# Beginning of a two-layer trunk: the first feature's modulation weights issued by ScalarE's queue beside SyncE's x tiles, the forget bias loaded behind the second half of x

## The chip, the core and the metric

The kernel runs on one core of a Trainium2 chip. The metric is device time in microseconds (us) of one launch.

## The reference

The trunk has two layers of width 1024 over 1024 tokens, all in float32. Layer 0 mixes tokens with forgetting attention, layer 1 with gated linear attention; each is followed by a SwiGLU. What stands at the beginning:

```
c_act = jax.nn.silu(c)
mod = c_act @ ada_w[i] + ada_b[i]
sh1, sc1, g1, sh2, sc2, g2 = jnp.split(mod, N_MOD, axis=-1)
h = modulate(rms_norm(x, norm1_g[i]), sh1, sc1)      # h * (1 + sc1) + sh1
proj = h @ w_in
q, k, v, f_logit = jnp.split(proj, [D, 2 * D, 3 * D], axis=-1)
log_f = jax.nn.log_sigmoid(f_logit + b_f)
cum = jnp.cumsum(log_f, axis=1).transpose(0, 2, 1)
```

So the first thing on TensorE that is of any size, the projections of layer 0, needs the normalised and modulated x, and this needs x, c, and shift and scale, which are products of c with 8 MB of `ada_w` (two blocks of 1024 x 1024).

## The kernel before

Every large matrix product is done as three: operands are split into a high and a low part (a cast on ScalarE for the high one, a subtraction on VectorE or GpSimd for the low one), and `mm3` (L240) issues high x high (L241), high x low (L242) and low x high (L243). The instructions of each engine stand in an order that a scheduler has chosen from its own model of the run; the code's order, priorities and the reuse of buffers bound it. So a change in the order of the code can move instructions on all engines.

**Tiles.** "Feature" d (0 to 7) is a block of 128 of the 1024 features; x tiles t (0 to 7) are blocks of 128 tokens, 512 KB each. The tokens are done in two halves: tiles 0 to 3 first, 4 to 7 next.

**Loads at the beginning.** `load_x` (L279) loads an x tile. `load_ada0(d)` (L284) loads what feature d needs of `ada_w`: two tiles `adas`, one for each half of the rows, each by two transfers of 256 KB (L288). c is loaded twice: as rows (L298) with other small vectors (L299 to L306), to be transposed by TensorE, and four times as a block of 32 x 32 (L294, `craw`) for later modulations (`cblk`, L325). `bf`, the forget bias (L311), is 64 bytes. `load_w16` (L215) loads the 16 columns of the forget logits, `load_w` (L198) a projection weight of 512 KB and splits it (L206 high on ScalarE, L209 low on GpSimd and VectorE). `ada_pair` (L361) loads, 128 KB at a time, what later modulations need.

**Queues.** SyncE (SP) issues all of these but the four blocks of c, which ScalarE (ACT) issues. The transfers of both engines take eight completion semaphores in turn, DMAHW0 to DMAHW7, in the order in which the scheduler places them: a transfer waits, on the engine that issues it, until the previous one on its semaphore has landed. An engine issues its transfers in its order, and on ScalarE arithmetic stands in the same order behind them.

**The first half.** `ss_half(0)` squares x (L458, ScalarE), makes the row scales and scales x (L469). For each d, `pre(d)` (L840) calls `ada0_mod(d)` (L474), `load_ada0(d + 3)` and `h_block(d, 0)`. `ada0_mod` forms shift and scale of a feature: for d = 0 to 2 four of the eight row blocks are products on TensorE (L481) and four accumulate on VectorE (L487, L489), for d = 3 to 7 all eight on VectorE; two matmuls with ones (L491, `mp`) sum the accumulated tile over its partitions; L492 and L342 turn the sum into `modc` and `amul`. `h_block` (L495) transposes x (L498, `xp`), modulates it on ScalarE (L500, `y`), casts the high part there (L502) and takes the low part (L503) on VectorE for even d, GpSimd for odd d. `first_k` (L508) does the forget logits (L510, L511, `fs`), and the first query and key projections (`qs`, `ks`); `first_v` (L829) the values (`vps`).

**Between the halves.** At d = 4 the loads of x tiles 4 to 7 are written, then `ss_half(1)`. `first_evac(0)` (L799) takes the logits out of PSUM (L223), applies bias, absolute value, exponential and, behind the second half, logarithm and a scan along the tokens; `v_split` (L163, L164) splits the values; `h_block(d, 1)` and `first_k(d, 1)` do the second half. The scan's result goes to memory and back, and attention starts with it.

Of the kernel before, what the change touches and what calls it, by code (L numbers as in the profile page):

```python
# [53 lines left out]
def trunk(ctx, tc, x, c, ada_w, ada_b, norm1_g, norm2_g, ffn_w_in, ffn_w_out,  # L54
          fox_w_in, fox_b_f, fox_w_out, gla_w_in, gla_w_a2, gla_b_a, gla_g_o,
          gla_w_out, final_g, out, dbg=None, stop=None):
    nc = tc.nc
# [51 lines left out]
    def psl(t, n=1):  # L109
        return slice(t * P, (t + n) * P)  # L110
# [167 lines left out]
    def load_x(t):  # L278
        nc.sync.dma_start(xt[t], x[0, psl(t), :])  # L279

    adaw = ada_w.rearrange("l (k p) (j d m) -> l p k j d m", p=P, j=6, m=P)
    araw = {}

    def load_ada0(d):  # L284
        for kh in range(2):
            t = adr([P, 4, 2, P], F32, f"adas{d}{kh}")
            for j in range(2):
                nc.sync.dma_start(t[:, :, j, :], adaw[0, :, 4 * kh:4 * kh + 4, j, d, :])  # L288
            araw[(d, kh)] = t

    craw = mrows[4][:, 0:32]
    cblk = cst.tile([P, 32], F32, name="cblk")
    for q in range(4):
        nc.scalar.dma_start(craw[32 * q:32 * q + 32], c[0].rearrange("(r s) -> r s", s=32))  # L294
    load_x(0)
    rows2 = mrows[1][0:32]
    nc.vector.memset(rows2, 0.0)
# [8 lines left out]
    nc.sync.dma_start(rows[112:128, :], norm2_g.rearrange("l (j p) -> (l j) p", p=P))  # L306
    load_x(2)
    load_x(3)
    load_ada0(0)
    bf = cst.tile([16, 1], F32, name="bf")  # L310
    nc.sync.dma_start(bf, fox_b_f.rearrange("o h -> h o"))  # L311
    W = fox_w_in[0]
    wf = load_w16(W[:, 3 * D:3 * D + 16], "fw", wst)
    wq0 = load_w(W[:, 0:P], "wq0", wst)
    wk0 = load_w(W[:, D:D + P], "wk0", wst)
    load_ada0(1)
    load_ada0(2)

    vps = mp0([P, 160], F32, "vps")
# [135 lines left out]
    def ss_half(hf):  # L455
        for t in range(4 * hf, 4 * hf + 4):
            sq = sqr([P, D], BF16, f"sq{t}")
            nc.scalar.activation(sq, xt[t], AF.Square, accum_out=ssx[:, t:t + 1])  # L458
        cs = slice(4 * hf, 4 * hf + 4)
        nc.vector.tensor_scalar(rstd[:, cs], ssx[:, cs], 1.0 / D, EPS, op0=ALU.mult, op1=ALU.add)  # L460
        nc.gpsimd.tensor_tensor(rstd[:, cs], rstd[:, cs], mhalf[:, 0:4], op=ALU.pow)
        for t in range(4 * hf, 4 * hf + 4):
            r = rstd[:, t:t + 1]
            if hf == 0 and t % 2 == 0:
                nc.vector.tensor_scalar(xt[t], xt[t], r, None, op0=ALU.mult)
            elif hf == 0 and t == 1:
                nc.scalar.activation(xt[t], xt[t], AF.Copy, scale=r)
            else:
                nc.gpsimd.tensor_scalar(xt[t], xt[t], r, 1.0, op0=ALU.mult, op1=ALU.mult)  # L469
# [38 lines left out]
    def first_k(d, hf, acc):  # L508
        ps = acc[0][1]
        nc.tensor.matmul(ps, wf[:, d, :], hT[d].hi[:, hsl(hf)], start=d == 0, stop=False)  # L510
        nc.tensor.matmul(ps, wf[:, d, :], hT[d].lo[:, hsl(hf)], start=False, stop=d == 7)  # L511
        for w, ps in acc[1:]:
            mm3(ps, w.hi[:, d, :], w.lo[:, d, :], hT[d].hi[:, hsl(hf)], hT[d].lo[:, hsl(hf)], d == 0, d == 7)
# [316 lines left out]
    def first_v(d):  # L830
        wv = wvs[0][d // 4]
        for tp in range(2):
            for i in range(2):
                ts_ = psl(2 * tp + i)
                p_, a_ = vacc[tp][:, i, :], (hT[d].hi[:, ts_], hT[d].lo[:, ts_])
                nc.tensor.matmul(p_, a_[0], wv.hi[:, d % 4, :], start=d == 0 and i == 0, stop=False)
                nc.tensor.matmul(p_, a_[0], wv.lo[:, d % 4, :], start=False, stop=False)
                nc.tensor.matmul(p_, a_[1], wv.hi[:, d % 4, :], start=False, stop=d == 7 and i == 1)

    def pre(d):  # L840
        ada0_mod(d)
        if d + 3 < 8:
            load_ada0(d + 3)
        h_block(d, 0)

    pre(0)
    for d in range(8):
        if d == 0:
            feed.depth = 1
            wvs[0] = [feed.next()]  # L850
        if d == 2:
            wvs[0].append(feed.next())
        if d < 7:
            pre(d + 1)
        first_k(d, 0, acc)
        if d >= VLAG:
            first_v(d - VLAG)
        if d == XD:
            for t in range(4, 8):
                load_x(t)  # L860
            ss_half(1)
    for d in range(8 - VLAG, 8):
        first_v(d)
# [1085 lines left out]
```

## Time and profile before

| | us |
|---|---|
| median of 3 runs | 2429.87 |
| lowest, highest | 2428.5, 2430.59 |
| profiled execution, its time | 2430.71 |
| its span | 2429.0 |
| TensorE busy | 2375.2 (98%) |
| VectorE busy | 1689.5 (70%) |
| ScalarE busy | 1192.6 (49%) |
| GpSimd busy | 1164.0 (48%) |

The span runs from the first to the last instruction that the profiler recorded. The mean granted clock of TensorE in it was 0.992 of full speed. In rows of the order of time, the columns are start and length (us), engine, line, operation, what is written and read by the program's names (buffer numbers left out), shape and count; in brackets how long the engine had waited, and for what. "SPq" is SyncE's queue of transfers, "PE" is TensorE. In rows by stretches of time the columns are the stretch, its sum, busy time and instructions of PE, its weight loads, VectorE (DVE), ScalarE (ACT) and GpSimd (POOL), then the granted clock of TensorE, the mean busy share of the DMA engines (of which more than one can count in a stretch that transfers enter and leave) and GB/s.

### The profile page before, as it was taken

What the parts mean: (1) busy time and instruction counts of PE and PEld (TensorE: products, weight loads), DVE (VectorE), ACT (ScalarE), POOL (GpSimd) and SP (SyncE); (2) the same over time, 40 slices, a digit from 0 to 9 for tenths busy, and PEclk for the clock granted to TensorE, in tenths of its full rate; (3) what the DMA queues carried; (4) which work ended last, traced back from release to release, by engine and by line L of the source; (5) the groups of instructions that cost most, each with busy time, mean ns of one, the idle gap of its engine ahead of it and who ended that gap; (6) DMA issues with size and microseconds to landing.
All of it is one profiled execution on the core that took longest, in us unless ns stands there. A gap on an engine that the chain in (4) does not pass through costs nothing.

```text
span 2429.0 us, 36104 instructions
## 1 busy us (share of the span) xinstructions
PE 2375.2 (98%) x12338; PEld 2019.5 (83%) x12338; DVE 1689.5 (70%) x2845; ACT 1192.6 (49%) x2286; POOL 1164.0 (48%) x1015
## 2 busy tenths in 40 slices
PE   7999999999999999999999999999999999999998
PEld 6788888878888888888888798898888888888888
DVE  6578777676687777766788545436587767666787
ACT  4656556666544444445324756654343334345325
POOL 3333333333337878753363544552335656653362
PEclk9999999999999999999999999999999999999999
DMA  9233333123326555457665334444325434347664
GB/s 271 80 105 113 94 108 113 62 88 120 118 96 192 180 167 171 156 187 262 229 204 168 83 114 117 126 126 156 109 84 186 152 135 155 128 169 258 231 209 148
DMA packets 329503, 362.40 MB, mean 149 GB/s; under 512 B 24476, under 2 KB 252984, under 8 KB 329320
## 3 DMA queue, kind: packets, MB, share of 16 engines
q1 hardware_dynamic: 329128, 360.09, 46.2%
q8 instruction: 97, 1.59, 0.3%
q14 instruction: 86, 0.70, 0.1%
q10 hardware_dynamic: 192, 0.02, 0.0%
HBM read 269.78 MB, written 90.24 MB: 148 GB/s over the span
## 4 chain that ended last, share of the span: by engine, by line
PE 78%; DVE 6%; DMA 6%; ACT 3%; issue 2%; POOL 2%; SPq 2%; DVEq 0%; POOLq 0%; ACTq 0%
PE p_b L241 16%; PE p_b L243 16%; PE p_b L242 16%; PE o_b L968 2%; PE t_b L954 2%; SPq L361 1%; DMA ad_s<-in_ada_w_dram 1%; PE qk_b L241 1%; PE qk_b L242 1%; PE qk_b L243 1%; DMA ada_s<-in_ada_w_dram 1%; PE s_b L923 1%; PE s_b L924 1%; PE vps_b L241 1%; PE vps_b L242 1%
## 5 line engine op out<-in xcount | busy, mean ns | idle before, releaser
L164 DVE TENSOR_TENSOR o_s<-xv_s,o_s 128x512 fp32r<-128x512 f32 (+1 forms) x376 | 333.4, 890 | 82.3 <-ACT o_s L163 81.3
L163 ACT CAST o_s<-xv_s 128x512 fp32r<-128x512 f32 (+1 forms) x376 | 217.9, 586 | 319.5 <-PE p_b L243 250.8
L934 POOL TENSOR_SCALAR lp_s<-lp_s,st 128x128 f32<-128x128 f32 (+7 forms) x128 | 98.5, 775 | 291.1 <-DVE st L933 273.1
L242 PE MATMUL p_b<-B,o_s 128*128 128x512 f32 x608 | 237.8, 391 | 0.0
L243 PE MATMUL p_b<-B,o_s 128*128 128x512 f32 x608 | 237.2, 391 | 0.0
L241 PE MATMUL p_b<-B,o_s 128*128 128x512 f32 x608 | 236.6, 392 | 0.0
L702 POOL TENSOR_TENSOR ex_s<-xv_s,xv_s 128x512 f32<-128x512 f32 (+1 forms) x64 | 86.4, 1350 | 270.2 <-DMA xv_s<-in_ffn_w_in_dram 108.3
L241 PE MATMUL p_b<-T,o_s 128*128 128x512 f32 x480 | 186.7, 389 | 0.0
L242 PE MATMUL p_b<-T,o_s 128*128 128x512 f32 x480 | 186.7, 389 | 0.0
L243 PE MATMUL p_b<-T,o_s 128*128 128x512 f32 x480 | 180.7, 389 | 0.0
L932 ACT ACTIVATE lp_s<-lp_s,st 128x128 f32<-128x128 f32 (+7 forms) x128 | 99.3, 776 | 76.7 <-DVE st L928 73.9
L241 PEld LDWEIGHTS p_b<-B,o_s 128*128 128x128 f32 x608 | 115.0, 189 | 23.8
L243 PEld LDWEIGHTS p_b<-B,o_s 128*128 128x128 f32 x608 | 114.7, 189 | 24.0
L242 PEld LDWEIGHTS p_b<-B,o_s 128*128 128x128 f32 x608 | 114.9, 189 | 23.7
L1306 DVE TENSOR_TENSOR ex_s<-ex_s,p_b 128x512 f32<-128x512 f32 x140 | 93.6, 680 | 31.8 <-PE p_b L243 31.7
L704 POOL TENSOR_TENSOR xv_s<-ex_s,xv_s 128x512 f32<-128x512 f32 (+1 forms) x64 | 85.9, 1342 | 52.3 <-DVE o_s L164 49.7
L163 ACT CAST pt_s<-t_b 128x512 fp32r<-128x512 f32 (+1 forms) x160 | 79.9, 548 | 62.5 <-PE t_b L954 61.6
L243 PEld LDWEIGHTS p_b<-T,o_s 128*128 128x128 f32 x480 | 90.1, 188 | 18.8
L241 PEld LDWEIGHTS p_b<-T,o_s 128*128 128x128 f32 x480 | 90.1, 188 | 18.7
L242 PEld LDWEIGHTS p_b<-T,o_s 128*128 128x128 f32 x480 | 90.1, 188 | 18.6
L164 DVE TENSOR_TENSOR pt_s<-t_b,pt_s 128x512 fp32r<-128x512 f32 (+1 forms) x160 | 96.5, 631 | 11.4 <-ACT pt_s L163 10.8
L968 PE MATMUL o_b<-pt_s,v_s 128*128 128x256 f32 x512 | 95.6, 295 | 5.9 <-DVE pt_s L164 4.2
(1950 smaller groups left out, 7494.7 us busy)
## 6 DMA issues: line engine op xcount, KB each, us to landing
xv_s<-in_ffn_w_in_dram SPq DMA_DIRECT2D x176, 256.0 KB, 3.3
hid_B<-x SPq DMA_DIRECT2D x70, 512.0 KB, 2.8
ad_s<-in_ada_w_dram SPq DMA_DIRECT2D x384, 64.0 KB, 2.0
hid_T<-x SPq DMA_DIRECT2D x36, 512.0 KB, 2.8
xv_s<-in_ffn_w_out_dram SPq DMA_DIRECT2D x96, 192.0 KB, 5.1
ada_s<-in_ada_w_dram SPq DMA_DIRECT2D x128, 128.0 KB, 2.7
xv_s<-in_ffn_w_out_dram SPq DMA_DIRECT2D x40, 256.0 KB, 2.8
T2o<-hid_T SPq DMA_DIRECT2D x18, 512.0 KB, 9.0
```

The costliest lines, as they stand in the source:

```text
L163: nc.scalar.copy(hi, src)
L164: nc.vector.tensor_sub(lo, src, hi.bitcast(F32))
L241: nc.tensor.matmul(ps, ah, bh, start=start, stop=False)
L242: nc.tensor.matmul(ps, ah, bl, start=False, stop=False)
L243: nc.tensor.matmul(ps, al, bh, start=False, stop=stop)
L702: nc.gpsimd.tensor_add(s1, a21, a22)
L704: nc.gpsimd.tensor_sub(a11, s1, a11)
L932: nc.scalar.activation(lp, lp, AF.Exp, bias=mcur, scale=-1.0, accum_out=st[:, qi, 2:3])
L934: nc.gpsimd.tensor_scalar(lp, lp, st[:, qi, 3:4], 1.0, op0=ALU.mult, op1=ALU.mult)
L954: nc.tensor.transpose(tp[:, i, :], lps[qi][:, psl(2 * b + jj)], ident)
L968: nc.tensor.matmul(ops, lv, pts[b][:, hl, 2 * jj:2 * jj + 2, :], start=j == 0 and hl == 0, stop=False)
L1306: nc.vector.tensor_add(d, d if src is None else dest(G, src), ps)
```

## The change

`load_ada0` gets a parameter for the engine that issues. The loads of feature 0 are issued by ScalarE, ahead of x tile 0 in the code, where the four block loads of c stood; these stand where feature 0's loads were, behind x tile 3, still on ScalarE's queue. The load of the bias goes behind x tiles 4 to 7 in the code, still on SyncE. Nothing is computed in another way. In the kernel after, lines from L294 to L857 stand one lower.

```
-    def load_ada0(d):
+    def load_ada0(d, dma=nc.sync.dma_start):
         for kh in range(2):
             t = adr([P, 4, 2, P], F32, f"adas{d}{kh}")
             for j in range(2):
-                nc.sync.dma_start(t[:, :, j, :], adaw[0, :, 4 * kh:4 * kh + 4, j, d, :])
+                dma(t[:, :, j, :], adaw[0, :, 4 * kh:4 * kh + 4, j, d, :])
             araw[(d, kh)] = t
...
-    for q in range(4):
-        nc.scalar.dma_start(craw[32 * q:32 * q + 32], c[0].rearrange("(r s) -> r s", s=32))
+    load_ada0(0, nc.scalar.dma_start)
     load_x(0)
...
     load_x(2)
     load_x(3)
-    load_ada0(0)
+    for q in range(4):
+        nc.scalar.dma_start(craw[32 * q:32 * q + 32], c[0].rearrange("(r s) -> r s", s=32))
     bf = cst.tile([16, 1], F32, name="bf")
-    nc.sync.dma_start(bf, fox_b_f.rearrange("o h -> h o"))
...
         if d == XD:
             for t in range(4, 8):
                 load_x(t)
+            nc.sync.dma_start(bf, fox_b_f.rearrange("o h -> h o"))
             ss_half(1)
```

The scheduler's order differs from before in the opening of the program, up to the first query tiles of attention, and in a few neighbours at the start of layer 1. Three places follow.

**SyncE's queue at the start**, with the semaphore that each transfer waits for (`mrows` are the small vectors, `xt_s_3` and `xt_s_4` x tiles 2 and 3). Before:

```order
L304 DMA mrows_s_88<-in_ada_b_dram 96x128 [waits DMAHW2_49]
L305 DMA mrows_s_88<-in_norm_g_dram 16x128 [waits DMAHW3_49]
L306 DMA mrows_s_88<-in_norm_g_dram 16x128 [waits DMAHW4_49]
L279 DMA xt_s_3_91<-in_x_dram 128x1024 [waits DMAHW5_49]
L279 DMA xt_s_4_92<-in_x_dram 128x1024 [waits DMAHW6_49]
L288 DMA adas_s_1_114<-in_ada_w_dram 128x4x128 [waits DMAHW7_49]
L288 DMA adas_s_1_114<-in_ada_w_dram 128x4x128 [waits DMAHW0_49]
```

After:

```order
L303 DMA mrows_s_88<-in_ada_b_dram 96x128 [waits DMAHW4_49]
L304 DMA mrows_s_88<-in_norm_g_dram 16x128 [waits DMAHW6_49]
L305 DMA mrows_s_88<-in_norm_g_dram 16x128 [waits DMAHW0_49]
L279 DMA xt_s_3_91<-in_x_dram 128x1024 [waits DMAHW1_49]
L279 DMA xt_s_4_92<-in_x_dram 128x1024 [waits DMAHW2_49]
L215 DMA fw_s_1_121<-in_fox_w_in_dram 128x8x16 [waits DMAHW3_49]
L198 DMA wq_s_2_127<-in_fox_w_in_dram 128x8x128 [waits DMAHW4_49]
```

And ScalarE's beginning after (before, it began with the four block loads of c, `mrows_s_88<-in_c_dram`, without waits, and a table load):

```order
L288 DMA adas_s_1_98<-in_ada_w_dram 128x4x128 x2
L288 DMA adas_s_2_101<-in_ada_w_dram 128x4x128 x2
L309 DMA mrows_s_88<-in_c_dram 32x32 [waits DMAHW1_49]
L309 DMA mrows_s_88<-in_c_dram 32x32 [waits DMAHW3_49]
L309 DMA mrows_s_88<-in_c_dram 32x32 [waits DMAHW5_49]
L309 DMA mrows_s_88<-in_c_dram 32x32 [waits DMAHW7_49]
L457 ACT_TABLE_LOAD
L457 ACTIVATE sq_s_1_208,ssx<-xt_s_1_89 128x1024
```

Semaphores 0, 3, 5 and 7 belong to the four weight loads, 1 and 2 to x tiles 0 and 1, and, from the second use on, 1 to the first block load of c: x tile 2 (`xt_s_3`) waits for that block, and ScalarE's arithmetic stands behind all four blocks. Further back on SyncE the first 128 KB piece of the next modulations (`ada020`, L360 after) stands ahead of feature 7's second pair of transfers, and the bias behind x tile 7.

**TensorE around feature 7's sum** (`mp_b_9<-ones,acc`). Before, it stood behind the low parts of feature 5's and a part of feature 6's work:

```order
L838 MATMUL vps_b_4_226<-wv_4h_s_3_364,h0l_193 128x256
L838 MATMUL vps_b_5_227<-wv_4h_s_3_364,h0l_193 128x256
L491 MATMUL mp_b_9_570<-ones,acc_571 128x1 x2
L836 MATMUL vps_b_5_227<-wv_4h_s_3_364,h0h_192 128x256
L837 MATMUL vps_b_5_227<-wv_4l_s_4_365,h0h_192 128x256
L838 MATMUL vps_b_5_227<-wv_4h_s_3_364,h0l_193 128x256
L498 MATMUL xp_b_9_674<-ident,xt_s_5_93 128x128
```

After, it stands ahead of them:

```order
L836 MATMUL vps_b_5_226<-wv_4l_s_4_364,h0h_189 128x256
L490 MATMUL mp_b_9_570<-ones,acc_571 128x1 x2
L510 MATMUL fs_b_1_222<-h0l_190,fw_s_1_123 128x512
L242 MATMUL qs_b_2_223<-h0l_190,wq0h_s_2_129 128x512
L243 MATMUL qs_b_2_223<-h0h_189,wq0l_s_3_130 128x512
L242 MATMUL ks_b_3_224<-h0l_190,wk0h_s_4_139 128x512
L243 MATMUL ks_b_3_224<-h0h_189,wk0l_s_5_140 128x512
```

The sum has moved forward by a part of feature 5's matmuls and all of feature 6's.

**ScalarE between the halves.** `y` and `h0h` are the modulated x and its high part, `ze_s_2<-fs_b_1` begins the evacuation of the first half's logits. Before, four features of the second half had their `y` ahead of it:

```order
L500 ACTIVATE y_s_86<-xp_b_9_674,modc,amul 128x512
L502 CAST h0h_194<-y_s_87 128x512
L500 ACTIVATE y_s_86<-xp_b_10_682,modc,amul 128x512
L502 CAST h0h_180<-y_s_86 128x512
L500 ACTIVATE y_s_87<-xp_b_11_698,modc,amul 128x512
L502 CAST h0h_182<-y_s_86 128x512
L500 ACTIVATE y_s_87<-xp_b_12_714,modc,amul 128x512
L502 CAST h0h_184<-y_s_87 128x512
L223 COPY ze_s_2_201<-fs_b_1_223 16x512
```

After, the first and the last rows of the same piece of work are:

```order
L499 ACTIVATE y_s_86<-xp_b_10_682,modc,amul 128x512
L223 COPY ze_s_2_200<-fs_b_1_222 16x512
L501 CAST h0h_179<-y_s_86 128x512
```

```order
L163 CAST v_s_2_669<-vps_b_5_226 128x4x64
L798 ACTIVATE ze_s_2_200<-zt_s_1_199,bf 16x512
L499 ACTIVATE y_s_87<-xp_b_11_698,modc,amul 128x512
L499 ACTIVATE y_s_87<-xp_b_12_714,modc,amul 128x512
L800 ACT_TABLE_LOAD
L800 ACTIVATE ze_s_2_200<-ze_s_2_200 16x512
L163 CAST v_s_1_664<-vps_b_4_225 128x4x64
L501 CAST h0h_183<-y_s_87 128x512
```

Two features of the second half have their `y` ahead of the evacuation now; `y` of feature 2 (`xp_b_11`) comes behind the first value casts and the absolute value, and its high part (`h0h_183`) behind a table load and an exponential.

More of the change, by code (lines that the diff above doesn't have):

```diff
@@ L282, in trunk, with load_ada0 @@
     araw = {}
-    def load_ada0(d):
+    def load_ada0(d, dma=nc.sync.dma_start):
         for kh in range(2):
@@ L287, in load_ada0 @@
             for j in range(2):
-                nc.sync.dma_start(t[:, :, j, :], adaw[0, :, 4 * kh:4 * kh + 4, j, d, :])
+                dma(t[:, :, j, :], adaw[0, :, 4 * kh:4 * kh + 4, j, d, :])
             araw[(d, kh)] = t
@@ L292, in trunk @@
     cblk = cst.tile([P, 32], F32, name="cblk")
-    for q in range(4):
-        nc.scalar.dma_start(craw[32 * q:32 * q + 32], c[0].rearrange("(r s) -> r s", s=32))
+    load_ada0(0, nc.scalar.dma_start)
     load_x(0)
@@ L308, in trunk @@
     load_x(3)
-    load_ada0(0)
+    for q in range(4):
+        nc.scalar.dma_start(craw[32 * q:32 * q + 32], c[0].rearrange("(r s) -> r s", s=32))
     bf = cst.tile([16, 1], F32, name="bf")
-    nc.sync.dma_start(bf, fox_b_f.rearrange("o h -> h o"))
     W = fox_w_in[0]
@@ L860, in trunk @@
                 load_x(t)
+            nc.sync.dma_start(bf, fox_b_f.rearrange("o h -> h o"))
             ss_half(1)
```

## The prediction

> **What bounds the kernel now.** I read the page first, then the opening 110 us by stretches, then SyncE's queue, ScalarE, VectorE and TensorE in order of time there, because the order of instructions differs only in those 110 us and, by a few neighbours, at the start of the second layer.
>
> ```profile
> span 2429.0 us, 36104 instructions
> PE 2375.2 (98%) x12338; PEld 2019.5 (83%) x12338; DVE 1689.5 (70%) x2845; ACT 1192.6 (49%) x2286; POOL 1164.0 (48%) x1015
> ```
>
> TensorE is busy nearly throughout: a microsecond won or lost in the opening shifts all that follows, and nothing behind it gives it back. The profiled execution took 2430.71 us, 1.7 more than its span; the median of the three runs is 2429.87, 0.84 below it. I add my sum to the median.
>
> Stretches of 5 us (last columns: granted clock, DMA share, GB/s):
>
> ```profile
> 5.00:10.00 5.00, 0.73 (x2) 0.36 (x2) 0.33 (x1) 3.50 (x7) 0.00 (x0) 1.00 0.45 125
> ...
> 25.00:30.00 5.00, 5.00 (x17) 4.32 (x18) 3.01 (x7) 0.00 (x0) 0.00 (x0) 1.00 1.22 290
> ```
>
> From about 9 us to 58 the DMA engines are full at some 290 GB/s; before that they idle for half of 5 to 10 us. What they carry last decides when the first half of the input is done:
>
> ```profile
> 49.76 8.52 DMA adas_s<-in_ada_w_dram
> ```
>
> This is feature 7's last weight tile, landing at 58.28. VectorE waits for it:
>
> ```profile
> 58.39 0.52 DVE L489 SCALAR_TENSOR_TENSOR acc<-adas_s,cact,acc 128x256 f32<-128x256 f32 x1 [2.54 <-DMA adas_s<-in_ada_w_dram]
> 58.83 0.95 DVE L209 TENSOR_TENSOR w_l_s<-w__s,w_h_s 128x256 fp32r<-128x256 f32 x1
> 59.70 2.61 DVE L489 SCALAR_TENSOR_TENSOR acc<-adas_s,cact,acc 128x256 f32<-128x256 f32 x2
> 62.24 0.68 DVE L503 TENSOR_TENSOR h0l<-y_s,h0h 128x512 fp32r<-128x512 f32 x1
> 62.84 1.26 DVE L489 SCALAR_TENSOR_TENSOR acc<-adas_s,cact,acc 128x256 f32<-128x256 f32 x1
> ```
>
> Then TensorE, feature 7's sum first; the other rows give the pitch of matmuls (0.23 us for 512 columns, 0.12 for 256) and two ends:
>
> ```profile
> 64.84 0.50 PE L491 MATMUL mp_b<-ones,acc 128*128 128x1 f32 x4
> ...
> 88.39 0.39 PE L510 MATMUL fs_b<-h0h,fw_s 128*128 128x512 f32 x1
> 88.62 0.39 PE L241 MATMUL qs_b<-h0h,wq0h_s 128*128 128x512 f32 x1
> ...
> 89.08 0.28 PE L241 MATMUL vps_b<-wv_0h_s,h0h 128*128 128x256 f32 x1
> 89.19 0.28 PE L242 MATMUL vps_b<-wv_0l_s,h0h 128*128 128x256 f32 x1
> ...
> 89.43 0.40 PE L511 MATMUL fs_b<-h0l,fw_s 128*128 128x512 f32 x1
> ...
> 103.66 0.77 PE L241 MATMUL qk_b<-h0h,w_h_s 128*128 128x512 f32 x1 [3.18 <-DVE v_s L164]
> ```
>
> The matmul at 89.43 closes the forget logits. Their chain through ScalarE and VectorE (evacuation, exponential, logarithm, scan) releases TensorE at 103.66, after 3.18 us idle. So **the end that counts is 89.43**; value matmuls behind it fill a shadow.
>
> **The change part by part.** 1. *Four weight loads (L288) leave SyncE's queue.*
>
> ```profile
> 0.80 0.85 SPq L279 DMA_DIRECT2D xt_s<-in_x_dram  x2
> ...
> 7.24 0.90 SPq L279 DMA_DIRECT2D xt_s<-in_x_dram  x2
> 8.17 2.68 SPq L288 DMA_DIRECT2D adas_s<-in_ada_w_dram  x4
> 10.90 1.60 SPq L311 DMA_DIRECT2D bf<-in_fox_b_f_dram  x1
> 12.55 0.42 SPq L215 DMA_DIRECT2D fw_s<-in_fox_w_in_dram  x1
> ```
>
> On paper the projection weights could issue at 8.17 instead of 12.55, 4.4 us earlier: 2.68 for the loads and 1.60 for the bias. But the stage is full of bytes, so what counts is 4 x 256 KB = 1.05 MB less in the stream, 3.6 us at 290 GB/s.
>
> 2. *The semaphores.* SyncE's waits before the second pair of x tiles:
>
> ```profile
> SPq L300 <- DMA mrows_s<-in_c_dram: 1.5, 1, 1.5
> SPq L304 <- DMA xt_s<-in_x_dram: 1.0, 1, 1.0
> ```
>
> L300 writes nothing that the c loads touch; it waits because the two queues take eight completion semaphores in turn, and a load waits for the previous load on its semaphore. In the new order tile x2 takes the semaphore of the first c load, which now stands on ScalarE's queue behind 1.05 MB of weights:
>
> ```profile
> adas_s<-in_ada_w_dram SPq DMA_DIRECT2D x32, 256.0 KB, 5.6
> ...
> ada_s<-in_ada_w_dram SPq DMA_DIRECT2D x8, 128.0 KB, 6.5
> ...
> mrows_s<-in_c_dram ACTq DMA_DIRECT2D x4, 4.0 KB, 4.2
> ```
>
> Even 4 KB took 4.2 us on that queue while the x tiles ran. Tile x1 had landed when L304 was released, at 5.95 by the wait that ends there; 1.05 MB more at 290 GB/s makes 9.5, and x2 goes out then instead of at 7.24: 2.3 us lost. Bounds: 8.6 if the two streams together reach 400 GB/s (1.4 lost), 11 if the weights are as slow beside x as the c loads were (3.8 lost). Gain minus loss, 1.3, between -0.2 and 2.2.
>
> The Trainium skill (DMA: Bandwidth & Descriptors, section "Issuing engines are not separate DMA queues") says that loads from several engines share the same 16 DMA engines and interleave, so that a second queue saves only issue time. By that rule the term would be the idle filled minus any new wait; the 4.2 us for 4 KB agrees.
>
> 3. *Ahead of the last tile.* The order now puts one 128 KB load of the next pair ahead of feature 7's last tile: 0.45 us at 290 GB/s. The bias behind x costs 0 to its old 1.60; it carries 64 bytes and the engines stay full, so I take 0.3. Left of the lead: 1.3 - 0.45 - 0.3, about **0.5 us** (from -2.2 to 1.8).
>
> 4. *ScalarE held at the start.* Each c load waits on ScalarE's own queue for an x or weight load, the last for the last weights, 9.5; only then does its arithmetic begin:
>
> ```profile
> 2.66 1.28 ACT L458 ACT_TABLE_LOAD   x1 [2.66 <-issue]
> 4.65 1.06 ACT L458 ACTIVATE sq_s<-xt_s 128x1024 bf16<-128x1024 f32 x1 [0.71 <-DMA xt_s<-in_x_dram]
> ...
> 12.52 1.06 ACT L458 ACTIVATE sq_s<-xt_s 128x1024 bf16<-128x1024 f32 x1 [0.23 <-DMA xt_s<-in_x_dram]
> ...
> 22.46 0.77 ACT L500 ACTIVATE y_s<-xp_b,modc,amul 128x512 f32<-128x512 f32 x1
> ...
> 31.98 0.78 ACT L500 ACTIVATE y_s<-xp_b,modc,amul 128x512 f32<-128x512 f32 x1 [8.10 <-DVE amul L342]
> ```
>
> Two table loads of 1.28 and four squares of 1.06 make 6.8, so the last square ends near 17 rather than 13.6, and everything that hangs on the row scales is 3 us late; y of feature 0 moves from 22.46 to about 25. Cover: ScalarE then stood 8.10 us before feature 1's y, which waits for weights. I take 0; without the cover it costs up to 2.5.
>
> 5. *TensorE's order.* Feature 7's sum is now ahead of feature 5's lower matmuls and all of feature 6's. Behind the landing the weight-low and h0l leave VectorE's chain, so four accumulations of 0.52 to 1.3 remain: 2.1 to 4.7 us; I take 3.2, so the sum runs at 58.28 - 0.5 + 3.4 = 61.2 instead of 64.84: 3.6 gained. But 13 more 512-column and 15 net more 256-column matmuls stand behind it: 13 x 0.23 + 15 x 0.12 = 4.8 lost. Net 1.2 lost.
>
> 6. *ScalarE's order at the second half.* Rows of before:
>
> ```profile
> 71.47 0.58 ACT L223 COPY ze_s<-fs_b 16x512 f32<-16x512 f32 x1
> ...
> 76.33 0.65 ACT L163 CAST v_s<-vps_b 128x256 fp32r<-128x256 f32 x2
> 76.86 0.80 ACT L500 ACTIVATE y_s<-xp_b,modc,amul 128x512 f32<-128x512 f32 x1
> ...
> 79.70 1.28 ACT L801 ACT_TABLE_LOAD   x1
> ...
> 81.78 0.61 ACT L502 CAST h0h<-y_s 128x512 fp32r<-128x512 f32 x1
> ```
>
> Before, four of the second half's eight h tiles were under way ahead of the evacuation at 71.47. Now two are, and h of feature 2 stands behind the evacuation, the sigmoid steps and a table load. From 71.47 to 76.33 are eight pieces of 0.6; nine such (5.4), two value casts and one absolute value (1.1), two y (1.5), the table load (1.28), an exponential (0.6), another cast (0.3) and h (0.6) make 10.7 us. TensorE closes the first half 17 matmuls of 512 columns, 24 of 256 and 8 transposes after feature 7's sum: 3.9 + 2.9 + 1.0 = 7.8, at 69.0; the copy follows at 69.4, and h of feature 2 at 80.1. Behind it TensorE still has 44 matmuls of 512, 12 of 256 and 8 transposes: 10.1 + 1.4 + 1.0 = 12.5, and ends at **92.6 instead of 89.43: 3.2 us late**. This takes in terms 3 and 5. Were the order on ScalarE harmless, the end would be at 89.43 + 1.2, so term 6 lies between 0 and 2.0.
>
> Sum: 2429.87 + 3.2 = 2433.1, which is 2433.9 against the profiled execution.
>
> **The rivals.** *A, the lead is kept and the new orders cost nothing:* the tail moves by the 1.05 MB less the 0.45, minus 3.1, if x2 need not wait for the c load and TensorE is as full as before: 2426.8. For it: the idle DMA share of 0.45; against it: the semaphore, and 4.8 us of matmuls behind feature 7. *B, the lead is spent and the orders do not matter:* weights, TensorE and ScalarE all come out as before, 2429.9; for it, VectorE is busy in that stage whatever the order; against it, the count behind h of feature 2. *C, slower by more than my sum:* the cover of term 4 fails. If x2 goes out after 10.5, the row scales are over 4 us late, feature 1's product is late too, and the tail of term 6 follows: 2433.1 + 2.5 = 2435.6. It decides from the landing of the last of the four loads: before 10 us it is hidden, after 10.5 it shows. *D, a cold clock:*
>
> ```profile
> 100.00:105.00 5.00, 1.82 (x8) 1.45 (x7) 5.00 (x10) 0.88 (x3) 0.00 (x0) 0.74 0.28 52
> ```
>
> After the 3.18 us idle the granted clock fell to 0.74 in this stretch. TensorE now stands at feature 7's sum for some 3 us (first-half work ends near 58.5); the same dip there, 0.26 of 5 us, costs 1.3: 2434.4. The Trainium skill (TensorE: Matmul & The Clock Gate, section "What's actually happening") says that an idle window of about 3.4 us halves the clock, which would make this term 1.7; the row agrees in kind, and which idle falls in a window is left to chance.
>
> **How the numbers follow.** Forecast 0.45, A 0.10, B 0.17, C 0.18, D 0.10. The range runs from just below A to past C and D with C's bound on the landing: 2426.3 to 2438.0. It leaves out about 0.06 on either side. A change of 0.2% is 4.86 us, about what a measurement of this kernel can tell from none. Faster by that needs 2425.0, 1.8 below A: 0.04. Slower by that needs 2434.7: C, half of D and a fifth of the forecast's own spread, 0.18 + 0.05 + 0.09 = 0.32. The same: 0.64.
>
> **What would show it.** Steps 2 and 4: SyncE issues x2 near 9.5 and ScalarE's first table load starts near 9.9. Step 3: the last weight tile lands between 57 and 58.5. Step 5: feature 7's sum near 61, behind an idle of 2 to 3 us. Step 6: the closing matmul of the forget logits near 92.6, after an idle before feature 2's second half. I am wrong if x2 issues before 8, if the last tile lands before 56, or if TensorE shows no idle at those two places.

## The result, and the profile after

Before: 2429.47 us median of 20 runs (2424.64 to 2430.89). After: 2434.86 us median of 20 runs (2430.14 to 2441.02). The ratio is 1.0025, with a 95% interval of 1.0019 to 1.003: the change costs 5.4 us by the medians and about 6 by the ratio, a little over the 0.2% that I had set as the bound of what can be told (the interval begins at 0.19%). The forecast was 2433.1, in a range of 2426.3 to 2438.0, with 0.64 for "within 0.2%" and 0.32 for slower: the time lies in the range, and the less likely of these two came.

The profiled execution after took 2431.38 us (span 2429.7), only 0.7 more than that of before. It is one of the fastest of its 20, and at 263 us from its start it is 5.0 us behind; where a part of that came back is shown at the end of this section.

SyncE's queue after, in order of time (start, length, line, what is loaded):

```profile
5.18 0.25 SPq L299 DMA_DIRECT2D mrows_s<-in_gla_b_a_dram  x1
...
9.33 0.31 SPq L305 DMA_DIRECT2D mrows_s<-in_norm_g_dram  x1
9.68 0.90 SPq L279 DMA_DIRECT2D xt_s<-in_x_dram  x2
```

and what it waited for there (total, times, longest):

```profile
SPq L299 <- DMA adas_s<-in_ada_w_dram: 2.8, 1, 2.8
SPq L305 <- DMA mrows_s<-in_gla_b_a_dram: 1.5, 1, 1.5
```

X tile 2 leaves at 9.68 instead of 7.24. The chain of semaphores is there, but it binds one step earlier than I had it: L299 waits 2.8 us for the first of the four weight loads, and then L305, ahead of x tile 2, for the 2 KB that L299 had sent 4 us earlier. ScalarE after:

```profile
9.73 1.28 ACT L457 ACT_TABLE_LOAD   x1 [9.73 <-DMA mrows_s<-in_c_dram]
...
23.60 0.78 ACT L499 ACTIVATE y_s<-xp_b,modc,amul 128x512 f32<-128x512 f32 x1 [2.87 <-PE xp_b L497]
```

It is held to 9.73, and the first `y` comes 1.1 us later than before (23.60, 22.46). Feature 7's last weight tile, from the chain that ended last (start of the transfer, length):

```profile
48.53 8.42 DMA adas_s<-in_ada_w_dram
```

It lands at 56.95, 1.3 us earlier than before. VectorE and TensorE behind it:

```profile
57.07 2.76 DVE L488 SCALAR_TENSOR_TENSOR acc<-adas_s,cact,acc 128x256 f32<-128x256 f32 x3 [0.22 <-DMA adas_s<-in_ada_w_dram]
...
59.87 1.22 DVE L488 SCALAR_TENSOR_TENSOR acc<-adas_s,cact,acc 128x256 f32<-128x256 f32 x1
```

```profile
61.23 0.58 PE L490 MATMUL mp_b<-ones,acc 128*128 128x1 f32 x4 [3.19 <-DVE amul L341]
...
70.65 0.48 PE L510 MATMUL fs_b<-h0l,fw_s 128*128 128x512 f32 x1
...
78.90 0.47 PE L241 MATMUL ks_b<-h0h,wk0h_s 128*128 128x512 f32 x1 [1.06 <-DVE KLB L638]
...
82.70 0.50 PE L509 MATMUL fs_b<-h0h,fw_s 128*128 128x512 f32 x1 [1.31 <-ACT h0h L501]
...
94.99 0.39 PE L510 MATMUL fs_b<-h0l,fw_s 128*128 128x512 f32 x1
```

The reader should see four things: TensorE stands 3.19 us at feature 7's sum; the first half's last logit matmul is at 70.65 (before: 69.88); two idles of 1.06 and 1.31 follow in the second half; and the closing matmul is at 94.99 instead of 89.43, **5.6 us late**. The stretch from the first half's last logit matmul to the closing one, for before and for after (stretch, length, then TensorE's busy time):

```profile
69.88:89.43 19.55, 19.55 (x109) 16.83 (x107) 7.33 (x13) 14.91 (x26) 5.17 (x4) 1.00 0.00 1
```

```profile
70.65:94.99 24.34, 21.53 (x117) 17.80 (x116) 8.00 (x14) 17.77 (x30) 5.15 (x4) 1.00 0.00 1
```

Before, TensorE is busy through all of its 19.55 us. After, the stretch is 24.34, of which 2.8 us are idle and 2.0 more are work: 27 transposes stand in it now instead of 16, and a matmul that follows a wait is longer. I call this stretch the tail, and what is ahead of it the head.

Of the 5.6 us, 5.0 are left at 263 us, past the first part of attention (the start of the same matmuls in both traces). At 300 us this one execution got a part back, where the clocks of the two traces differ. These are the rows of before and of after (last columns: granted clock, DMA share, GB/s):

```profile
300.00:305.00 5.00, 3.38 (x13) 2.98 (x14) 3.98 (x13) 1.92 (x5) 0.80 (x1) 0.54 0.51 148
305.00:310.00 5.00, 5.00 (x28) 4.39 (x28) 1.81 (x9) 2.26 (x7) 1.71 (x3) 0.78 0.29 102
```

```profile
300.00:305.00 5.00, 3.73 (x22) 2.81 (x20) 4.64 (x13) 2.45 (x6) 0.00 (x0) 1.00 0.57 155
305.00:310.00 5.00, 3.25 (x23) 2.93 (x24) 4.47 (x15) 1.94 (x5) 0.80 (x1) 1.00 0.49 147
```

The execution of before had a clock of 0.54 there, that of after 1.00; the distance falls from 5.0 to 3.0 within these 10 us. Behind that it moves both ways (3.6 at 700 us, before ahead; 2.0 at 1395 us, after ahead), and 0.7 is left at the end. So my sentence that nothing behind the opening gives a microsecond back does not hold for a single execution. It holds for the medians as far as can be told: they lie 5.4 apart.

### The profile page after: what moved, and what is told of

Same layout as the page of the kernel before. It is cut to its first block, busy times and chain, and to the rows that moved or that the text cites. A ratio compares the mean times of both kernels' runs of the same rounds, so it can differ in the third digit from the quotient of the medians.

```text
span 2429.7 us, 36108 instructions
## 1 busy us (share of the span) xinstructions
PE 2372.9 (98%) x12338; PEld 2018.4 (83%) x12338; DVE 1705.0 (70%) x2845; ACT 1196.5 (49%) x2286; POOL 1168.8 (48%) x1015
## 4 chain that ended last, share of the span: by engine, by line
PE 80%; DMA 5%; DVE 5%; ACT 4%; issue 2%; POOL 2%; SPq 1%; ACTq 0%; DVEq 0%; POOLq 0%
PE p_b L242 16%; PE p_b L241 16%; PE p_b L243 16%; PE o_b L968 2%; PE t_b L954 2%; PE qk_b L241 1%; PE qk_b L242 1%; DMA ad_s<-in_ada_w_dram 1%; PE qk_b L243 1%; SPq L360 1%; PE s_b L923 1%; PE s_b L924 1%; DMA ada_s<-in_ada_w_dram 1%; PE vps_b L241 1%; PE vps_b L242 1%
## 5 line engine op out<-in xcount | busy, mean ns | idle before, releaser
L164 DVE TENSOR_TENSOR o_s<-xv_s,o_s 128x512 fp32r<-128x512 f32 (+1 forms) x376 | 339.6, 907 | 76.1 <-ACT o_s L163 74.1
```

The source lines that it names most:

```text
L164: nc.vector.tensor_sub(lo, src, hi.bitcast(F32))
```

## The experiments

Two theories. **O**: the scheduler's new order of the engines costs the time, by the stall at feature 7's sum (step 5) and by ScalarE's order between the halves (step 6). **L**: the loads cost it, since x tile 2 leaves 2.4 us later and ScalarE is held.

To tell them apart, an order has to be had without the loads that led to it. The engines trace the same instructions in before and after, so a table of positions can hold one kernel's opening in the other's order. At the end of `trunk`:

```
FIXED = {"P": [(0, 10), (12, 13), ...], "A": [...], "D": [...], "G": [...]}
for e, spans in FIXED.items():
    mine = [... traced instructions of engine e, without transfers ...]
    o = [mine[k] for a_, b_ in spans for k in range(a_, b_)]
    for i0, i1 in zip(o, o[1:]):
        tc.add_manual_dep(i1, i0.name, <issue order only, no wait>)
```

It covers the first 395 instructions of TensorE, 62 of ScalarE, 109 of VectorE and the part of GpSimd's that differs; nothing waits for more than before.

All runs in one table: time ratio to the kernel before on the same chip with its interval; then from each trace the first half's last logit matmul, the closing one, and the tail between them (us).

| run | loads | order | ratio (95%) | first half's last | closing | tail |
|---|---|---|---|---|---|---|
| before | old | old | 1 | 69.88 | 89.43 | 19.55 |
| after | new | new | 1.0025 (1.0019 to 1.003) | 70.65 | 94.99 | 24.34 |
| e1 | old | new | 1.0029 (1.0017 to 1.0041) | 72.59 | 96.90 | 24.31 |
| e2 | new | old | 1.0 (0.9991 to 1.0009) | 71.48 | 91.03 | 19.55 |
| e3 | weights alone | new | 1.0033 (1.002 to 1.0046) | 70.60 | 94.91 | 24.31 |
| e4 | bias alone | old | 0.9996 (0.9987 to 1.0006) | 72.23 | 91.73 | 19.50 |
| e5 | c on GpSimd | scheduler's | 1.001 (1.0001 to 1.0019) | 68.14 | 92.21 | 24.07 |
| e6 | c on GpSimd | old | 0.9996 (0.9986 to 1.0005) | 69.80 | 89.30 | 19.50 |
| e7 | old | head old, tail new | 1.0019 (1.001 to 1.0028) | 69.15 | 92.70 | 23.55 |
| e8 | old | head new, tail old | 1.0023 (1.001 to 1.0035) | 75.36 | 98.18 | 22.82 |
| e9 | old | old, feature 7 | 0.9987 (0.9978 to 0.9996) | 70.17 | 89.69 | 19.52 |
| e10 | c on GpSimd | old, feature 7 | 0.9996 (0.9987 to 1.0006) | 70.49 | 89.99 | 19.50 |
| e11 | new | new | 1.002 (1.0011 to 1.0029) | 69.43 | 93.73 | 24.30 |
| e12 | old | old, feature 7 | 0.9995 (0.9986 to 1.0004) | 69.98 | 89.50 | 19.52 |

**e1, the old loads in the new order.** Edit: the table of after's order in the kernel before.

> All transfers as before; the instructions of TensorE, ScalarE, VectorE and GpSimd in the opening are held in the order that they have after the change. If the order is the cause (theory O), the time is 5 us above before (2434 to 2436), feature 7's sum on TensorE stands near 61 behind an idle of 2 to 3 us, and the closing matmul of the forget logits comes near 95. If the loads are the cause (theory L: x tile 2 leaves 2.4 us later, ScalarE is held), this is within 1 us of before, and the closing matmul stays near 89.4.

Measured: 2437.82 against 2431.08, ratio 1.0029 (1.0017 to 1.0041). TensorE:

```profile
63.17 0.58 PE L491 MATMUL mp_b<-ones,acc 128*128 128x1 f32 x4 [2.93 <-DVE amul L342]
...
72.59 0.47 PE L511 MATMUL fs_b<-h0l,fw_s 128*128 128x512 f32 x1
...
96.90 0.39 PE L511 MATMUL fs_b<-h0l,fw_s 128*128 128x512 f32 x1
```

The order alone, with x tile 2 back at 7.33, gives the whole loss and the same tail. In the new order the old loads are even the later ones, by 1.9 us at the closing matmul (96.90 against 94.99, both with a cold clock behind the sum). The sum is later than I expected (63.17, not 61), since the last tile keeps its old landing.

**e2, the new loads in the old order.** Edit: the table of before's order in the kernel after.

> The loads as after the change; the four engines held in the order that they had before it. Theory O: within 1.5 us of before (2428 to 2431); x tile 2 still leaves near 9.7, the closing matmul of the forget logits comes near 89 to 90.5. Theory L: 4 to 6 us above before, the closing matmul near 95.

Measured: 2430.53 against 2431.08, ratio 1.0 (0.9991 to 1.0009).

```profile
65.94 0.50 PE L490 MATMUL mp_b<-ones,acc 128*128 128x1 f32 x4
...
71.48 0.40 PE L510 MATMUL fs_b<-h0l,fw_s 128*128 128x512 f32 x1
...
91.03 0.40 PE L510 MATMUL fs_b<-h0l,fw_s 128*128 128x512 f32 x1
```

X tile 2 leaves at 10.01, ScalarE is held as in after, and no loss can be told; the tail is 19.55 again. **Theory L falls** as the cause of the 6 us. A smaller cost of the loads is not excluded: the interval is 2 us wide on either side, and in this trace the closing matmul is 1.6 us later than in before (half a microsecond beyond my 90.5), with the clock at 1.00 from 55 us on.

**e3 and e4, the two parts of the change.** Edit of e3: the bias stays ahead of the projection weights. Edit of e4: the bias alone moves.

```
-    nc.sync.dma_start(bf, fox_b_f.rearrange("o h -> h o"))
...
             for t in range(4, 8):
                 load_x(t)
+            nc.sync.dma_start(bf, fox_b_f.rearrange("o h -> h o"))
```

> The change without its second part: feature 0's weights on ScalarE's queue, the c blocks behind them, the bias at its old place. The order of the engines is that of the whole change. Both theories: 2434 to 2436, as after; the bias is worth less than 0.5 us. If the bias is what costs, this is at before's 2429.5.

> Only the bias moves behind x tiles 4 to 7; all else, the order of the engines too, as before. Theories O and L: within 0.5 us of before. If the bias has a part in the cost, up to 2 us above.

Measured: e3 2438.54, ratio 1.0033 (1.002 to 1.0046); e4 2431.12, ratio 0.9996 (0.9987 to 1.0006). The weights make the loss, since they make the new order; the bias is worth nothing that can be told. The trace of e4 shows that the cold clock is not a matter of the new order alone: TensorE stood idle for 2.60 us shortly before the sum there, the clock was 0.66 from 65 to 70 us, and the closing matmul came at 91.73.

**e5 and e6, c off ScalarE's queue.** Edit, in the kernel after; e6 has the table of before's order as well:

```
     for q in range(4):
-        nc.scalar.dma_start(craw[32 * q:32 * q + 32], ...)
+        nc.gpsimd.dma_start(craw[32 * q:32 * q + 32], ...)
```

> The change, with the four block loads of c issued by GpSimd, whose queue takes other semaphores, in place of ScalarE: no x tile waits for them any more and ScalarE's arithmetic is not held behind them. x tile 2 leaves near 7.3 instead of 9.7. The scheduler's order is still of the new kind (feature 7's sum early, two y of the second half ahead of the evacuation). Theory O (the order costs): 2 to 6 us above before. Theory L (the semaphore costs): at or below before, 2426 to 2430.

> As the run before, with the four engines held in the order of the kernel before. If SyncE's stream sets the opening's end, it keeps the whole lead of 1.05 MB: the last weight tile lands 2 to 3.5 us earlier, and the time is 1.5 to 3.5 us below before. If the lead is lost in the engines' work behind the landings, it is within 1 us of before.

Measured: e5 2433.97 against 2430.67, ratio 1.001 (1.0001 to 1.0019); e6 2428.78, ratio 0.9996 (0.9986 to 1.0005). e5 is as theory O has it, at its low end: the order is again of the new kind, with a tail of 24.07. X tile 2 left at 8.81 and 8.85, not at 7.3 as I had put down. SyncE's waits in e6:

```profile
SPq L299 <- DMA adas_s<-in_ada_w_dram: 2.9, 1, 2.9
SPq L303 <- DMA xt_s<-in_x_dram: 1.0, 1, 1.0
...
SPq L304 <- DMA adas_s<-in_ada_w_dram: 0.4, 1, 0.4
SPq L279 <- DMA adas_s<-in_ada_w_dram: 0.4, 1, 0.4
```

So c's place behind the weights is worth 0.9 us of the 2.4 (9.68 to 8.81); the rest is that the weight loads themselves hold semaphores that SyncE's next loads need. In e6 the last tile was issued at 48.0 and landed 8.1 us later, at 56.1, 2.1 us ahead of before, and yet its closing matmul is at 89.30, within 0.13 of before. The lead is lost behind the landing, on VectorE first:

```profile
56.92 0.47 DVE L488 SCALAR_TENSOR_TENSOR acc<-adas_s,cact,acc 128x256 f32<-128x256 f32 x1
58.09 1.27 DVE L209 TENSOR_TENSOR w_l_s<-w__s,w_h_s 128x256 fp32r<-128x256 f32 x1 [0.70 <-ACT w_h_s L206]
59.28 1.83 DVE L488 SCALAR_TENSOR_TENSOR acc<-adas_s,cact,acc 128x256 f32<-128x256 f32 x2
61.04 0.68 DVE L502 TENSOR_TENSOR h0l<-y_s,h0h 128x512 fp32r<-128x512 f32 x1
61.64 1.26 DVE L488 SCALAR_TENSOR_TENSOR acc<-adas_s,cact,acc 128x256 f32<-128x256 f32 x1
```

No row there waits for the tile any more (before, 2.54 us); a weight's low part, which waits for ScalarE, stands in the chain instead. The chain ends at 62.9, against 64.1 before: 1.2 us of the 2.1 are left, and 0.6 at the sum (64.26, 64.84):

```profile
64.26 0.50 PE L490 MATMUL mp_b<-ones,acc 128*128 128x1 f32 x4
```

The sum waits for nothing there. It comes 1.4 us behind the end of VectorE's chain, because TensorE is still busy with what stands ahead of it (5.00 of 5 us from 60 to 65; before, 3.55). So neither the landing nor VectorE sets the sum in e6. The last 0.5 us goes behind the sum, where TensorE waits 0.59 us for x that GpSimd scales and 0.43 us for ScalarE (before, 0.52 in all).

C's place behind the weights shows in the traces of the old order: closing matmul at 91.03 with c on ScalarE's queue (e2), at 89.30 without (e6), both with the clock at 1.00. The times of the two cannot tell them apart.

**e7 and e8, one part of the new order at a time**, with the loads of before. Edit of e7: ScalarE's table takes its first 40 positions from before and the others from after; the other engines follow freely. Edit of e8: TensorE's first 252, ScalarE's first 40 and VectorE's first 96 positions are those of after, the others those of before; GpSimd's are not held.

> Loads as before; the first half's order as before; only ScalarE's order between the halves and behind is that of after (two y ahead of the evacuation, feature 2's high part behind the table load), and TensorE's second half follows from it. If ScalarE's order at the second half is the main term (theory O with step 6 as the larger): 3 to 4.5 us above before, an idle of over 1 us ahead of the second half's feature 2, and the closing matmul near 93. If the stall at feature 7's sum and the cold clock behind it are (theory O with step 5 as the larger): under 1.5 us above before.

> Loads as before; the first half's order on TensorE, ScalarE and VectorE as after (feature 7's sum ahead of features 5's low parts and 6), everything behind as before. Step 6 as the larger: 0.5 to 2 us above before, an idle of 2 to 3 us ahead of the sum near 61 to 63, the closing matmul near 91. Step 5 as the larger: 3 to 5 us above before, the closing matmul over 93.

Measured: e7 2436.13 against 2430.67, ratio 1.0019 (1.001 to 1.0028).

```profile
72.69 0.50 PE L510 MATMUL fs_b<-h0h,fw_s 128*128 128x512 f32 x1 [0.36 <-ACT h0h L502]
76.59 0.47 PE L241 MATMUL ks_b<-h0h,wk0h_s 128*128 128x512 f32 x1 [1.05 <-DVE KLB L639]
80.39 0.50 PE L510 MATMUL fs_b<-h0h,fw_s 128*128 128x512 f32 x1 [1.30 <-ACT h0h L502]
```

The three idles of after's second half are there, with an old head: sum at 64.42, no stall at it, closing matmul at 92.70. ScalarE's order at the second half, with what the scheduler then makes of the other engines' order, makes 3.3 us of the loss at that place. That is the cause that step 6 named, and more than the 2.0 us that it allowed.

e8: 2435.55, ratio 1.0023 (1.001 to 1.0035), and a closing matmul at 98.18, far from my 91. The hybrid made a new fault:

```profile
66.37 0.53 PE L511 MATMUL fs_b<-h0l,fw_s 128*128 128x512 f32 x1 [3.07 <-POOL h0l L503]
...
79.03 0.66 PE L498 MATMUL xp_b<-ident,xt_s 128*128 128x128 f32 x4 [0.20 <-ACT y_s L500]
```

TensorE waits 3.07 us more, for a low part that GpSimd, whose order was free, made late; and the old ScalarE order puts four `y` ahead of the evacuation, whose transposes the new TensorE order has only at 79. So e8 does not price the head. It shows that the two orders cannot be mixed at will: in the new head the transposes come late, and then the evacuation may no longer stand behind four `y`.

**e9, e10 and e12, VectorE's chain shortened.** Since a part of e6's lead was lost on VectorE, and TensorE in before waits 1.45 us for VectorE's low part at 62.97, feature 7's second tile goes to TensorE, eight one-column matmuls more and four accumulations less; old order, with the table shifted by these. e9 and e12 are the same kernel with the loads of before, e10 has those of e6.

```
-    NPE = (4, 4, 4, 0, 0, 0, 0, 0)
+    NPE = (4, 4, 4, 0, 0, 0, 0, 4)
...
         npe = NPE[d]
+        on_pe = list(range(4, 8)) if d == 7 else list(range(npe))
+        on_dve = [k for k in range(8) if k not in on_pe]
...
-            for k in range(npe):
+            for k in on_pe:
                 nc.tensor.matmul(mp[:, j:j + 1], part(k)[:, j, :], cact[:, k:k + 1], ...)
...
```

> Loads and order of the kernel before; the only change: the four row blocks of feature 7's second weight tile are multiplied on TensorE (eight matmuls of one column, about 1 us) and no longer accumulated on VectorE. If VectorE's chain behind the last landing sets the end of the first half, feature 7's sum comes 2 us or more earlier (near 62 to 63 instead of 64.8), the closing matmul near 87, and the time is 1.5 to 3 us below before. If the landing itself sets it, the sum moves by under 1 us and the time stays within 1 us of before.

> The loads of the run with c on GpSimd (weights of feature 0 on ScalarE's queue, bias late), the order of the kernel before, and feature 7's second tile on TensorE. If VectorE ate the lead of those loads, the sum comes near 60 to 61, the closing matmul near 85 to 86, and the time is 3 to 5 us below before. If not, it is as the run without the move, within 1.5 us of before.

> The kernel with feature 7's second tile on TensorE and the loads and order of before, once more. If its gain is real: 1 to 4 us below before again. Feature 7's sum again near 64; where the clock stays at 1.0 behind it, the closing matmul comes near 88 to 88.5, else near 89.7. If the first result was chance: within 1 us of before.

Measured: e9 2428.0 against 2430.3, ratio 0.9987 (0.9978 to 0.9996); e12 2427.75 against 2429.7, ratio 0.9995 (0.9986 to 1.0004); e10 2428.46, ratio 0.9996 (0.9987 to 1.0006). In e9, VectorE now waits for TensorE's sum, and TensorE is busy without a break from 57 to 65 us:

```profile
64.43 0.16 DVE L494 TENSOR_TENSOR modc<-mp_b,vec 128x2 f32<-128x2 f32 x1 [6.09 <-PE mp_b L493]
```

The sum comes 1.0 us earlier (63.81), the closing matmul not at all (89.69). Between them the clock fell, in e9 and again in e12:

```profile
65.00:70.00 5.00, 4.57 (x23) 3.79 (x22) 0.75 (x1) 4.23 (x7) 2.04 (x3) 0.66 0.34 107
```

```profile
65.00:70.00 5.00, 4.56 (x23) 3.93 (x23) 0.76 (x1) 4.03 (x7) 2.18 (x2) 0.66 0.34 99
```

Of the gain of 2 us that I expected, TensorE's own work took one and the clock the other: from the sum to the closing matmul e9 takes 25.88 us, e10, the same matmuls with the clock at 1.00, 24.55. e9's interval ends below 1 and e12's does not (the medians are 2.3 and 2.0 us lower), so no version here is shown to beat the kernel before.

e10 missed what I expected if VectorE ate the lead: the sum came at 65.44, not at 60 to 61, and the closing matmul at 89.99, not at 85 to 86. TensorE is busy from 60 to 65 us there too, and the work ahead of the sum is 1.6 us later than in e9 (feature 5's first logit matmul at 56.55 against 54.90). So the lead of the new loads does not reach the work ahead of the sum; what holds that work was not followed further.

**e11, the changed kernel again.**

> The changed kernel once more, for a second trace. 4 to 7 us above before. The tail from the end of the first half to the closing matmul is again near 24.3 us, and the head varies by the cold clock behind feature 7's sum: up to 1.7 us less where the clock stays at 1.0.

Measured: 2436.33 against 2430.3, ratio 1.002 (1.0011 to 1.0029). Its TensorE rows:

```profile
61.56 0.58 PE L490 MATMUL mp_b<-ones,acc 128*128 128x1 f32 x4 [1.81 <-DVE amul L341]
...
69.43 0.47 PE L510 MATMUL fs_b<-h0l,fw_s 128*128 128x512 f32 x1
...
93.73 0.39 PE L510 MATMUL fs_b<-h0l,fw_s 128*128 128x512 f32 x1
```

and the stretches behind the sum, in the first execution and in this one:

```profile
60.00:65.00 5.00, 3.77 (x19) 3.53 (x20) 3.11 (x5) 1.58 (x3) 4.94 (x5) 0.77 0.22 69
65.00:70.00 5.00, 5.00 (x29) 4.43 (x29) 0.00 (x0) 1.22 (x2) 2.04 (x3) 0.89 0.00 0
```

```profile
60.00:65.00 5.00, 3.44 (x22) 3.12 (x23) 3.41 (x7) 1.40 (x2) 5.00 (x4) 1.00 0.28 82
65.00:70.00 5.00, 5.00 (x35) 4.57 (x34) 0.03 (x1) 2.12 (x4) 2.31 (x4) 1.00 0.00 0
```

The same instructions, from the sum to the first half's last logit matmul: 9.42 us with the clock at 0.77 and 0.89, 7.87 at 1.00. Both stretches hold 53 matmuls and no idle. The cold clock's price is 1.55 us, shown by one kernel against itself. e1 and e3, with the same order, give the same two lengths, 9.42 and 7.87: the clock fell in two of the four traces of this order. The tails are 24.34 and 24.30.

## Why the prediction was right, point by point

The time lies 1.8 us above the forecast, and the change is 5.4 us against a forecast of 3.2; the mechanism was the forecast's. Step 6 was too small, and the cold clock was left out of the sum.

- **Steps 1 to 3, the lead.** X tile 2 left at 9.68 (forecast 9.5). The last tile landed at 56.95, a lead of 1.3 us against my 0.5, just outside "57 to 58.5". The semaphore bound at L305, on a 2 KB load, and not at the first block of c; e6 shows that c's place accounts for 0.9 us of the 2.4 only.
- **Step 4, ScalarE held.** Table load at 9.73 (forecast 9.9), first `y` 1.1 us later instead of 2.5. As the cause of the loss the hold falls: e2 has the same hold and, within 2 us, the time of before. Rival C's condition, x tile 2 out after 10.5, was not met. That the hold costs nothing is not shown: in the old order it goes with 1.6 us at the closing matmul (e2), in the new order the kernel that has it is ahead of the one that has not (94.99, e1 96.90).
- **Step 5, the sum.** 61.23 behind an idle of 3.19 (forecast 61.2, 2 to 3). That the place fits is luck: the tile landed 0.8 us earlier than forecast, and VectorE's chain took 4.3 us from landing to sum where I had 3.4. Its four accumulations alone took 4.0 and not 3.2; my upper bound of 4.7 was also added up wrongly, four times 1.3 being 5.2. Rival A's gain did not show: even with 2.1 us of lead at the landing, e6 is 0.13 us ahead at the closing matmul, and its time cannot be told from before's.
- **Step 6, ScalarE at the second half.** From the evacuation's copy to the closing matmul I had 69.4 to 92.6, 23.2 us; measured 71.97 to 94.99, 23.0. e7 shows that this order makes most of the loss by itself (ratio 1.0019). The bound that I had put on the term, "between 0 and 2.0", was too tight. From the sum to the closing matmul, in before, in after and in e11 (stretch, length, then TensorE's busy time):

```profile
64.84:89.43 24.59, 24.06 (x141) 20.64 (x139) 8.50 (x16) 18.87 (x32) 8.40 (x9) 1.00 0.08 22
```

```profile
61.23:94.99 33.76, 30.95 (x166) 26.39 (x167) 9.95 (x17) 20.73 (x34) 10.90 (x10) 0.95 0.01 2
```

```profile
61.56:93.73 32.17, 29.39 (x167) 24.97 (x168) 9.97 (x17) 20.68 (x34) 10.92 (x10) 1.00 0.01 1
```

  By step 5's count this stretch is 24.59 + 4.8 = 29.4 us. With the clock at 1.00 (e11) TensorE is busy for just that, and stands for 2.8 more: the term is 2.8. The tails differ by more, 4.8 (24.34 against 19.55), since 2.0 us of work, transposes for the most part, moved from the head to the tail.
- **The step that failed** is the place where the first half ends: copy at 69.4 in the forecast, 71.97 in the trace. ScalarE after shows one part of it:

```profile
70.49 1.45 ACT L499 ACTIVATE y_s<-xp_b,modc,amul 128x512 f32<-128x512 f32 x2 [4.24 <-PE xp_b L497]
71.97 0.58 ACT L223 COPY ze_s<-fs_b 16x512 f32<-16x512 f32 x1
```

Two `y` of the second half stand ahead of the copy, and wait for transposes that TensorE has at 70.07; I had let the copy follow the last logit matmul by 0.4, which would be 71.05; it follows at 71.97, 0.9 us late. This lateness is what step 6 lacks, 2.8 against 2.0. The other part is the 1.55 us of cold clock: I had made it a rival (D, 1.3 us, chance 0.10) in place of the forecast, but the stall that it needs was a part of the forecast itself. 92.6 + 0.9 + 1.55 = 95.05; measured 94.99. This adds up the one trace. e11 has no cold clock and closes at 93.73, and how often the clock falls in the 20 runs is not known, so the share of the 1.8 us that is the clock's stays open. Rival B falls by e1 and e2: the order matters, and the loads do not by an amount that the times can tell. What the stall at the sum (step 5) costs by itself is open too, since e8 does not price it.

By the Trainium skill (DMA: Bandwidth & Descriptors, section "Issuing engines are not separate DMA queues") the loads of several engines interleave on the same DMA engines, and a second queue saves issue time alone. The traces agree where the engines are full (20 to 25 us: 298 GB/s before, 290 after); what the second queue filled is the idle of 5 to 10 us (125 GB/s before, 232 after). The Trainium skill (TensorE: Matmul & The Clock Gate, section "What's actually happening") gives an idle window of about 3.4 us as what turns the clock down. Here the clock fell behind shorter idles of 3.19 us (after), 2.93 (e1), 2.60 (e4) and 2.36 (e5), and did not behind 2.69 (e3) and 1.81 (e11): the length of the one idle does not decide it.

## What to carry to other kernels

Where a scheduler writes the order, a few loads that change their queue can rewrite the order of hundreds of instructions (here 321 of the first 395 positions on TensorE hold another one); price the new order, by the wait that each engine's next row is queued behind, before the load. Hold the old order with the new loads and the new order with the old loads: these two runs tell which of them the time belongs to, down to the width of their intervals. A stall that a forecast contains can bring a cold clock along, as in two of four traces here; give it a share in the sum, and do not set it apart as a rival.

## What the runs showed of the hardware that was not expected

- **Small transfers beside large ones.** 2 KB that SyncE sent at 5.18 held up SyncE until 9.33, while 1 MB of weights and the x tiles moved; a queue that takes its semaphores in turn with another queue's large loads waited for them even with loads that touch nothing of theirs (2.8 us at L299; 2.9 in e6).
- **The clock fell without an idle.** In e9 and e12 TensorE's rows have no idle over 0.64 us from 50 to 65 us, and the granted clock is 0.66 in 65 to 70. What stands ahead in e9 are ten matmuls of one column, from 62.10 to 64.25 (each shows as two in the rows):

```profile
62.10 1.84 PE L483 MATMUL mp_b<-cact,adas_s 128*128 128x1 f32 x16
63.81 0.58 PE L493 MATMUL mp_b<-ones,acc 128*128 128x1 f32 x4
```

Whether such matmuls count as little work for the clock was not tried by itself; e10 has them too and kept 1.00.
- **VectorE beside GpSimd.** In before, one accumulation of 128 x 256 takes 0.48 us from 49.4 to 54.4 us, where GpSimd is idle, and 1.23 to 1.35 us from 59.70 to 64.1, where GpSimd scales x (L469, from 59.48 on). The one at 58.39 took 0.52 beside another GpSimd instruction (L209), so a busy GpSimd is not enough for it. That the scaling is the reason was not tried apart.
